# A decoder layer with 32 experts on one core: four late experts for three, earlier loads for the last norms, and 8 KB buffers

## The chip, the cores and the metric

The kernel runs on one core of a Trainium2 chip. The metric is the device time of one execution in microseconds. Three executions of the kernel before took 1423.0, 1424.0 and 1429.07 us; the median is 1424.0 us. TensorE is called PE, VectorE DVE, ScalarE ACT, GpSimd POOL and SyncE SP. SP issues the plain loads and stores; POOL issues the indirect ones (gathers and scatters by row index).

## The reference

The layer works on 1024 tokens of width 1024 in float32. First come a gated linear recurrence and a sliding-window attention over projections of x, mixed and normalised; their result is x1. Then comes the part that the change touches, cut here to what matters:

```
x = layer_norm(ALPHA*x + merged @ w_out)                      # x1
# each token: the best of 4 groups, then the best 2 of its 8 experts
h = silu(xb @ w_gate[e]) * (xb @ w_up[e])                     # per expert, 512 wide
y[token] += (h @ w_down[e]) * weight
x = layer_norm(ALPHA*x + y)                                   # the output
```

A token is in two experts of one group, so the last experts of different groups (7, 15, 23, 31) share no token.

## The kernel before

**Order.** The stages are attention and projections, the linear recurrence, the mixing with the first norm and the router, and the experts. From the mixing on, the order on each engine is the order in which the program is written out (all_order); every engine works in order and waits where an operand or a buffer isn't ready.

**Experts.** Each expert has at most 128 tokens in its first pass. Its weights come in 12 pieces: four of gate, four of up (each 2 x 128 rows of 512) and four of down (128 rows of 1024). first_pieces lists them for all experts: gate and up of expert e+1 come ahead of down of expert e, 384 pieces in all; the numbers of experts below are places in ORDER, so 29, 30 and 31 are the three of LAST. moe (from line 1238) walks over the pieces: at step i it splits piece i+3 (halve), does what has been put down for step i, multiplies piece i and issues one more load (fetch). A split gives a high and a low part: ACT casts (line 97), DVE subtracts (line 98). A product of split parts is three passes of PE (lines 102 to 104); a product of unsplit ones is one float32 matmul, which the trace shows as two passes (line 1165). The pieces from gate of expert 31 on are unsplit (first_whole).

**Loads.** fetch issues pieces in their order on SP. 29 are issued ahead; each later one waits until the piece eight before it has landed (DEEP, after). Loads, splits and the tiles of the end use one set of 36 buffers of 4 KB per partition (q4).

**Results.** turn_x gathers and transposes an expert's tokens; turn_h transposes its silu product hh. result scales the two halves of down's product and adds them to zd in memory by an indirect scatter with addition (line 1068); zd begins as x1. PSUM has four banks for products (mm): two for gate and up, two for down.

**The end.** final is put down for the piece after down of expert 28 and three more: it loads the norm's gain and shift (line 908), then block i of zd (z, line 1287) at step first + i, once all scatters into zd have landed. Eight steps later it puts the norm of block i down, 1.75 steps apart: a sum on ACT (line 1296), a square on ACT (line 1320), then gain on DVE with a power on POOL (lines 678, 679, 1324) and shift on DVE (line 1327) in the next two steps, and the store of the block. For each expert in LAST, finish takes the rows of zd that rows gathered (zf), adds the expert's product to them (line 1340), norms them in the same way and writes them over the stored blocks by index, after all eight stores (line 1343).

Of the kernel before, what the change touches and what calls it, by code (L numbers as in the profile page):

```python
# [23 lines left out]
LAST = (15, 23, 31)  # L24
# [36 lines left out]
class Builder:  # L61
# [5 lines left out]

    S2 = {"ob", "as", "aph", "apl", "ach", "acl", "oT", "hq", "hk", "hl", "hv", "hg", "hkd", "hkT", "hqb", "hst", "hE", "hS", "hsq", "ho",
          "rxT", "rlT", "hh", "hth", "htl"}
    NQ = 36  # L70
    NX = 9
    NRAW = 29
    LA = 3

    def __init__(self, tc, aps):
        self.tc, self.nc, self.a = tc, tc.nc, aps

    def tile(self, shape, dt, tag, bufs, name=None):
        name = name or tag
        if tag in self.S2:  # L80
            tag, bufs = "s2", self.n2
        pool = self.base if tag in ("q4", "st2", "base") else self.sb
# [4 lines left out]
    def q4(self, shape, dt=F32, name="q4"):  # L87
        return self.tile(shape, dt, "q4", self.NQ, name)

# [6 lines left out]
    def split(self, hi, lo, src, eng=None):  # L96
        self.nc.scalar.copy(hi, src)  # L97
        (eng or self.nc.vector).tensor_sub(lo, src, hi.bitcast(F32))  # L98

# [61 lines left out]
    def load_x(self, half, j):  # L161
        raw = self.q4([128, 2, 512], name="xr")
        self.nc.sync.dma_start(raw, self.a["xt"][half, j])
        return raw

    def split_x(self, half, raws):

        self.xh.append([])
        self.xl.append([])
        for raw in raws:  # L170
            h, l = self.q4([128, 2, 512], F32R, "xh"), self.q4([128, 2, 512], F32R, "xl")
            self.split(h, l, raw)
            self.xh[half].append(h)
            self.xl[half].append(l)
            yield
# [8 lines left out]
    def wload_half(self, c0, q):  # L184
        raw = self.q4([128, 4, 256], name=f"wr{c0}")
        self.nc.sync.dma_start(raw, self.a["w_in"][c0 // 256, q])
        return raw
# [4 lines left out]
    def wsplit_half(self, raw):  # L192
        h = self.q4([128, 4, 256], F32R, "wh")
        l = self.q4([128, 4, 256], F32R, "wl")
        self.split(h, l, raw)
        return h, l
# [45 lines left out]
    def att_proj(self):  # L242
# [11 lines left out]
        self.aq = [self.q4([128, 4, 256], name=f"aq{i}") for i in range(4)]  # L254
# [32 lines left out]
        self.ak = self.q4([128, T], name="ak")  # L287
# [394 lines left out]
    def mixing_loads(self):  # L682

        nc = self.nc
        self.stages, self.late_stages = {}, {}
        self.wab, self.ot, self.gates = {}, {}, {}
        wv = [self.a[nm].rearrange("(k p) c -> p k c", p=128) for nm in ("w_a", "w_b")]

        def load_wab(jt, when):
            raw = self.q4([128, 2, 4, 128], name="wab")  # L690
            for i in range(2):
                nc.sync.dma_start(raw[:, i], wv[i][:, :, jt * 128:jt * 128 + 128])
            self.at(2 * when, lambda: self.halves(self.wab, jt, raw), True)

        def load_o(b, half, nm, j):
            raw = self.q4([128, 2, 512], name=f"o{nm}")
            d = self.obd if nm == "b" else self.oad
            nc.sync.dma_start(raw, d.rearrange("k p t -> p k t")[:, 2 * j:2 * j + 2, half * 512:half * 512 + 512])
# [15 lines left out]
    def halves(self, dst, key, raw, eng=None):  # L714
        h, l = self.q4(raw.shape, F32R, "h"), self.q4(raw.shape, F32R, "l")
        self.split(h, l, raw, eng)
        dst[key] = h, l
# [23 lines left out]
    def mixing(self):  # L741
# [27 lines left out]
        def load_wo(b, p):  # L769
            raw = self.q4([128, 2, 512], name="wo")  # L770
            c, kp = p // 4, p % 4
            nc.sync.dma_start(raw, wov[:, 2 * kp:2 * kp + 2, c * 512:c * 512 + 512])
            self.at(2 * b + 2, lambda: halves(wo, p, raw, nc.gpsimd))
# [5 lines left out]
        def branch(half, jt):  # L779
            pss = []  # L780
            h, l = wab.pop(jt)
            for b, nm in enumerate("ab"):
                ps = self.bank("mm")
                for k in range(4):
                    oh, ol = ot[nm, k // 2]
                    self.mm3(ps, h[:, b, k], l[:, b, k], oh[:, k % 2], ol[:, k % 2], k == 0, k == 3)
                pss.append(ps)
                if b == 0:
                    yield
            if jt % 2 == 0:  # L790
                mg[jt // 2] = self.q4([128, 2, 512], F32R, "mh"), self.q4([128, 2, 512], F32R, "ml")
# [71 lines left out]
        for b in range(24, 31):  # L863
            for _ in range(2 if b % 2 else 1):
                at(before, b, lambda b: self.fetch())
# [3 lines left out]
        while tick < 2 * len(main) or stages or self.late_stages:  # L869
# [19 lines left out]
            if tick >= 2 * len(main) - 1:  # L889
                for _ in range(4 if tick < 2 * len(main) + 1 else 2):  # L890
                    self.fetch(True)
# [179 lines left out]
    def first_pieces(self):  # L1071
# [14 lines left out]
        self.first_whole = self.pieces.index((NE - 1, "w_g", 0))  # L1086
        self.raws, self.fetched = {}, []

    def whole(self, e, m):

        return self.pieces.index((e, m, 0)) >= self.first_whole

    def fetch(self, first=False):

        n = len(self.fetched)
        if n >= len(self.pieces) or first and n >= self.NRAW:
            return
        e, m, k = self.pieces[n]
        x = ORDER[e]
        if m == "w_d":  # L1100
            r = self.q4([128, 1, D], name="er")
            ins = self.nc.sync.dma_start(r, self.a[m][x].rearrange("(k p) c -> p k c", p=128)[:, k:k + 1])
        else:
            r = self.q4([128, 2, 512], name="er")
            ins = self.nc.sync.dma_start(r, self.a[m][x, k])
        if n >= self.DEEP:
            self.after(ins, self.fetched[n - self.DEEP])
        self.fetched.append(ins)
        self.raws[n] = r

    DEEP = 8
# [109 lines left out]
    def halve(self, i):  # L1221
        if i >= len(self.pieces):
            return
        e, m, k = self.pieces[i]
        raw = self.raws.pop(i)
        if i >= self.first_whole:
            self.V["w", e, m, k] = raw, None
            return
        h = self.q4(raw.shape, F32R, name="eh")
        l = self.q4(raw.shape, F32R, name="el")  # L1230
        self.split(h, l, raw)
        self.V["w", e, m, k] = h, l
# [5 lines left out]
    def moe(self):  # L1238
# [18 lines left out]
        self.final(at[NE - len(LAST) - 1, "w_d", 3] + 3)  # L1257
        for i in range(n):
# [9 lines left out]
            self.fetch()  # L1268
# [6 lines left out]
    def final(self, first):  # L1275
# [9 lines left out]
        def load(i):  # L1285
            z = self.q4([128, D], name="z")
# [3 lines left out]
        def rows(e):  # L1290
            self.zf[e] = self.q4([128, D], name="zf")
# [11 lines left out]
        for i in range(8):  # L1303
            self.step(first + i, lambda i=i: load(i))
            self.step(first + 8 + 1.75 * i, lambda i=i: self.norm2(self.zs[i], sums(i), lambda: store(i)))
        for j in range(len(LAST)):
            self.step(first + 8 + j, lambda j=j: rows(NE - len(LAST) + j))
        self.stored = int(first + 8 + 1.75 * 7) + 4

    def norm2(self, z, s, then):  # L1310
# [8 lines left out]
        def square():  # L1319
            nc.scalar.activation(self.q4([128, D], name="w"), z, AF.Square, bias=m, accum_out=v)  # L1320
# [59 lines left out]
    def more(self, e):  # L1380
# [16 lines left out]
        for nm in ("w_g", "w_u"):  # L1397
            ps = self.bank("mm")
            for k in range(8):
                w = self.st2()  # L1400
                nc.sync.dma_start(w, self.a[nm][bass.ds(e, 1), k // 2].rearrange("o p i c -> (o p) i c")[:, k % 2])
# [11 lines left out]
        wv = self.a["w_d"][bass.ds(e, 1)].rearrange("o (k p) c -> p (o k) c", p=128)  # L1413
        for j in range(2):
            ps = self.bank("mm")
            for k in range(4):
                w = self.st2()
                nc.sync.dma_start(w, wv[:, k, j * 512:j * 512 + 512])
# [37 lines left out]
def gate_up(w):  # L1456

    return np.ascontiguousarray(w.reshape(NE, 4, 2, 128, 512).transpose(0, 1, 3, 2, 4))


def arrays(inputs):
# [15 lines left out]
        "w_g": gate_up(f["w_exp_gate"][0]),  # L1477
        "w_u": gate_up(f["w_exp_up"][0]),
        "w_d": f["w_exp_down"][0],
# [18 lines left out]
```

## Time and profile before

| | |
|---|---|
| median of three executions | 1424.0 us |
| the profiled execution | 1423.78 us |
| its span, first to last instruction | 1421.9 us |
| PE busy | 1359.1 us (96%) |
| DVE busy | 1058.2 us (74%) |
| ACT busy | 792.3 us (56%) |
| POOL busy | 239.6 us (17%) |
| moved by DMA | 327.68 MB, 230 GB/s over the span |
| loads of expert weights | 384 of 512 KB |

Busy shares are means over stages with different limits. In 40 slices of the span PE is at 9 tenths or more in nearly all; the last three slices read 8, 4 and 4. The DMA engines read 9 from slice 25 on, and 9, 7 and 2 in the last three. A matmul's end is modelled, so busy PE can hold short waits; the distance between the starts of neighbouring passes is the better measure.

### The profile page before, as it was taken

How to read it: one execution, taken by the hardware profiler on the slowest of the kernel's cores; microseconds unless marked ns; L12 is line 12 of the kernel's file. 1: busy time of each engine (PE TensorE's matmuls, PEld its weight loads, DVE VectorE, ACT ScalarE, POOL GpSimd, SP SyncE). 2: the span in 40 equal slices, each digit the busy share in tenths (PEclk: the TensorE clock that was granted, in tenths of full speed). 3: DMA queues.
4: the chain of work that ended last, by engine and by line, in shares of the span. 5: the costliest groups of instructions: out<-in, count | busy, mean ns of one | idle time of the engine just before them, and what ended most of it. 6: DMA issues, size and time to landing. Idle time of an engine off the chain costs nothing. (4 is left out here: it accounts for less than half of the span.)

```text
span 1421.9 us, 20450 instructions
## 1 busy us (share of the span) xinstructions
PE 1359.1 (96%) x7162; PEld 1128.3 (79%) x7162; DVE 1058.2 (74%) x1654; ACT 792.3 (56%) x1282; POOL 239.6 (17%) x160
## 2 busy tenths in 40 slices
PE   7999999999999999999998999999999999999844
PEld 5888899988888888788787888888888888888721
DVE  4268977876666764857747889999999999999635
ACT  4367555434444442412201778888888888888533
POOL 0001221210010000410001112222222222222123
PEclk9999999999999999999999999999999999999967
DMA  6124223253334323774557899999999999999972
GB/s 254 56 89 156 88 92 105 67 173 116 126 108 136 111 88 103 240 252 137 174 195 277 314 361 369 370 359 349 360 349 359 357 359 360 360 359 361 370 264 95
DMA packets 142554, 327.68 MB, mean 230 GB/s; under 512 B 18614, under 2 KB 59702, under 8 KB 142448
## 3 DMA queue, kind: packets, MB, share of 16 engines
q1 hardware_dynamic: 132800, 308.78, 60.4%
q0 software_dynamic: 9648, 17.57, 4.8%
q8 instruction: 57, 0.93, 0.3%
q14 instruction: 49, 0.40, 0.1%
HBM read 291.43 MB, written 52.43 MB: 242 GB/s over the span
## 5 line engine op out<-in xcount | busy, mean ns | idle before, releaser
L98 DVE TENSOR_TENSOR el<-er,eh 128x1024 fp32r<-128x1024 f32 x368 | 436.5, 1221 | 53.7 <-ACT eh L97 38.1
L97 ACT CAST eh<-er 128x1024 fp32r<-128x1024 f32 x368 | 368.9, 1053 | 100.6 <-PE mm L103 83.5
L102 PE MATMUL mm<-xh,wh 128*128 128x512 f32 x480 | 198.3, 413 | 8.3 <-ACT wh L97 7.3
L102 PE MATMUL mm<-eh,xh 128*128 128x512 f32 x496 | 196.4, 396 | 0.0
L103 PE MATMUL mm<-el,xh 128*128 128x512 f32 x496 | 196.2, 395 | 0.0
L104 PE MATMUL mm<-eh,xl 128*128 128x512 f32 x496 | 196.1, 395 | 0.0
L103 PE MATMUL mm<-xl,wh 128*128 128x512 f32 x480 | 188.4, 393 | 0.8 <-DVE xl L98 0.8
L104 PE MATMUL mm<-xh,wl 128*128 128x512 f32 x480 | 189.0, 394 | 0.0
L104 PEld LDWEIGHTS mm<-eh,xl 128*128 128x128 f32 x496 | 93.2, 188 | 22.6
L103 PEld LDWEIGHTS mm<-el,xh 128*128 128x128 f32 x496 | 93.2, 188 | 22.3
L102 PEld LDWEIGHTS mm<-eh,xh 128*128 128x128 f32 x496 | 93.2, 188 | 22.3
L102 PEld LDWEIGHTS mm<-xh,wh 128*128 128x128 f32 x480 | 91.1, 190 | 24.2 <-ACT wh L97 7.3
L104 PEld LDWEIGHTS mm<-xh,wl 128*128 128x128 f32 x480 | 90.6, 189 | 20.6 <-DVE wl L98 0.8
L1064 POOL DMA_INDIRECT xg<-x1d,gi x32 | 58.1, 1814 | 279.3 <-PE pb L1127 236.3
L103 PEld LDWEIGHTS mm<-xl,wh 128*128 128x128 f32 x480 | 91.1, 190 | 16.0 <-DVE xl L98 1.4
L102 PE MATMUL mm<-eh,hth 128*128 128x512 f32 x240 | 100.2, 418 | 0.0
L1068 POOL DMA_INDIRECT zd<-y,gi x29 | 69.9, 2411 | 156.5 <-ACT y L1218 156.5
L104 PE MATMUL mm<-eh,htl 128*128 128x512 f32 x240 | 94.8, 395 | 0.0
L103 PE MATMUL mm<-el,hth 128*128 128x512 f32 x240 | 94.8, 395 | 0.0
L102 PE MATMUL mm<-wh,xh 128*128 128x256 f32 x256 | 73.1, 285 | 0.0
L104 PE MATMUL mm<-wh,xl 128*128 128x256 f32 x256 | 72.4, 283 | 0.0
L103 PE MATMUL mm<-wl,xh 128*128 128x256 f32 x256 | 72.4, 283 | 0.0
(257 smaller groups left out, 2566.6 us busy)
## 6 DMA issues: line engine op xcount, KB each, us to landing
er<-w_g SPq DMA_DIRECT2D x128, 512.0 KB, 12.5
er<-w_u SPq DMA_DIRECT2D x128, 512.0 KB, 12.5
er<-w_d SPq DMA_DIRECT2D x128, 512.0 KB, 12.0
wr<-w_in SPq DMA_DIRECT2D x38, 512.0 KB, 4.4
gated<-st SPq DMA_DIRECT2D x32, 256.0 KB, 2.1
st<-gated SPq DMA_DIRECT2D x32, 256.0 KB, 2.7
xr<-xt SPq DMA_DIRECT2D x8, 512.0 KB, 7.6
wab<-w_a SPq DMA_DIRECT2D x16, 256.0 KB, 3.7
```

The source lines that it names most:

```text
L97: self.nc.scalar.copy(hi, src)
L98: (eng or self.nc.vector).tensor_sub(lo, src, hi.bitcast(F32))
L102: mm(out, lh, rh, start=start, stop=False)
L103: mm(out, lh, rl, start=False, stop=False)
L104: mm(out, ll, rh, start=False, stop=stop)
L1064: self.nc.gpsimd.indirect_dma_start(to, None, rows, bass.IndirectOffsetOnAxis(ap=self.column(self.gi, e), axis=0), bounds_check=T - 1, oob ...
L1068: self.nc.gpsimd.indirect_dma_start(self.zd, bass.IndirectOffsetOnAxis(ap=idx, axis=0), y, None, bounds_check=T - 1, oob_is_err=False, com ...
```

## The change

- LAST holds 7, 15, 23, 31, so four experts (places 28 to 31) are finished by norm and indirect write, and 28 scatter into zd.
- Buffers are 18 of 8 KB (q8) for 36 of 4 KB. A 4 KB tile with a pair key shares a buffer with the next of the same key; a split's high and low part share one; before, each had its own.
- Expert weights lie in memory in blocks of 1 MB, 8 KB per partition, and a load brings two pieces. 14 loads are issued ahead for 29 of half the size; a load waits for the fourth before it in place of the eighth.
- Unsplit are gate, up and down of expert 31 and gate and up of 30; down of 30 is split.
- final starts after down of expert 27, at that piece. Blocks of zd are loaded from first + 6, that is among the last four weight loads, rows are gathered from first + 6, norms start at first + 14 and stand 3 steps apart. The sums' and squares' outputs that nobody reads go to x4 tiles.
- Six loads of 1 MB are issued late in the mixing, where ten of 512 KB were.

The core of the diff:

```
-LAST = (15, 23, 31)
+LAST = (7, 15, 23, 31)
-    NQ = 36
+    NQ = 18
-    NRAW = 29
+    NRAW = 14
+    def q4(self, shape, pair, dt=F32):
+        if pair in self.pairs:
+            t = self.pairs.pop(pair)[:, 1024:2048]
+        else:
+            t = self.pairs[pair] = self.q8([128, 2048], dt, str(pair[0]))
+            t = t[:, 0:1024]
+        return self.shaped(t, shape)
+    def halved(self, src, eng=None):
+        hi, lo = self.parts(src.shape)
+        self.split(hi, lo, src, eng)
+        return hi, lo
+    def parts(self, shape):
+        t = self.q8([128, 2048], F32R, "hl")
+        return self.shaped(t[:, 0:1024], shape), self.shaped(t[:, 1024:2048], shape)
...
-        return self.pieces.index((e, m, 0)) >= self.first_whole
+        return e == NE - 1 or e == NE - 2 and m != "w_d"
...
-        if n >= len(self.pieces) or first and n >= self.NRAW:
+        if 2 * n >= len(self.pieces) or first and n >= self.NRAW:
...
+        e, m, k = self.pieces[2 * n]
+        r = self.q8([128, 2, D] if m == "w_d" else [128, 4, 512], name="er")
+        ins = self.nc.sync.dma_start(r, self.a[m][ORDER[e], k // 2])
...
-    DEEP = 8
+    DEEP = 4
...
-        self.final(at[NE - len(LAST) - 1, "w_d", 3] + 3)
+        self.final(at[NE - len(LAST) - 1, "w_d", 3])
...
-            self.fetch()
+            if i % 2:
+                self.fetch()
...
-            nc.scalar.activation(self.q4([128, D], name="w"), self.zs[i], AF.Copy, accum_out=s)
+            nc.scalar.activation(self.x4(name="w"), self.zs[i], AF.Copy, accum_out=s)
...
-            self.step(first + i, lambda i=i: load(i))
-            self.step(first + 8 + 1.75 * i, lambda i=i: self.norm2(self.zs[i], sums(i), lambda: store(i)))
+            self.step(first + 6 + i, lambda i=i: load(i))
+            self.step(first + 14 + 3 * i, lambda i=i: self.norm2(self.zs[i], sums(i), lambda: store(i)))
...
-            self.step(first + 8 + j, lambda j=j: rows(NE - len(LAST) + j))
-        self.stored = int(first + 8 + 1.75 * 7) + 4
+            self.step(first + 6 + j, lambda j=j: rows(NE - len(LAST) + j))
+        self.stored = first + 14 + 3 * 7 + 3
...
+def blocks(w):
+    n = 2048 // w.shape[2]
+    return np.ascontiguousarray(w.reshape(NE, 2, n, 128, w.shape[2]).transpose(0, 1, 3, 2, 4))
```

## Rows read from the trace of the kernel before

**Rows 1.** Busy time by stretches of the span; the first line names the columns.
```profile
core 0: us, PE busy (x) PEld busy (x) DVE busy (x) ACT busy (x) POOL busy (x), PEclk, DMA share, GB/s
800.00:905.00 105.00, 105.00 (x486) 85.47 (x485) 94.84 (x92) 85.35 (x104) 20.04 (x10) 1.00 1.00 364
905.00:1346.00 441.00, 441.00 (x2052) 359.43 (x2051) 394.99 (x386) 355.94 (x433) 104.80 (x49) 1.00 0.99 359
1346.00:1369.70 23.70, 0.57 (x4) 0.14 (x2) 0.15 (x1) 2.92 (x6) 0.00 (x0) 0.61 0.99 378
1369.70:1375.00 5.30, 5.30 (x7) 2.21 (x8) 3.33 (x6) 4.23 (x8) 3.31 (x2) 0.50 0.17 70
...
1406.00:1421.90 15.90, 0.03 (x1) 0.00 (x0) 5.47 (x9) 1.24 (x2) 4.30 (x5) 0.60 0.13 48
```

**Rows 2.** Timeline of POOL, 1305 to 1345: start, duration, line, operation [idle before].
```profile
1312.88 2.47 POOL L1068 DMA_INDIRECT zd<-y,gi  x1 [5.00 <-ACT y L1218]
1330.87 1.57 POOL L1068 DMA_INDIRECT zd<-y,gi  x1 [15.52 <-ACT y L1218]
```

**Rows 3.** Timeline of SP's queue: issues of weight loads and of z.
```profile
905.12 5.41 SPq L1105 DMA_DIRECT2D er<-w_g  x4
...
1327.88 4.81 SPq L1105 DMA_DIRECT2D er<-w_g  x4
...
1341.13 11.78 SPq L1102 DMA_DIRECT2D er<-w_d  x8
...
1356.34 9.19 SPq L1287 DMA_DIRECT2D z<-zd  x8
```

**Rows 4.** Timeline of ACT, 1338 to 1372.
```profile
1339.88 1.05 ACT L97 CAST eh<-er 128x1024 fp32r<-128x1024 f32 x1 [1.94 <-DMA er<-w_d]
1366.50 1.06 ACT L1296 ACTIVATE w<-z 128x1024 f32<-128x1024 f32 x1 [25.57 <-DMA z<-zd]
...
1369.08 1.05 ACT L1136 COPY xh<-pb 128x512 f32<-128x512 f32 x2
```

**Rows 5.** Timeline of PE, 1324 to 1329 and from 1365 on.
```profile
1328.29 0.40 PE L102 MATMUL mm<-eh,xh 128*128 128x512 f32 x1
1328.99 0.40 PE L102 MATMUL mm<-eh,xh 128*128 128x512 f32 x1
...
1369.69 6.75 PE L1165 MATMUL mm<-er,xh 128*128 128x512 f32 x9 [23.13 <-ACT xh L1136]
...
1386.15 5.31 PE L1165 MATMUL mm<-er,hth 128*128 128x512 f32 x12
1395.10 0.80 PE L1149 MATMUL pb<-const,hh 128*128 128x128 f32 x4 [3.64 <-DVE fv L678]
```

**Rows 6.** Groups by line: whole span, then 1340 to 1422; busy us, mean ns, idle before.
```profile
L98 DVE TENSOR_TENSOR el<-er,eh 128x1024 fp32r<-128x1024 f32 x368 | 436.5, 1221 | 53.7 <-ACT eh L97 38.1
...
L679 POOL TENSOR_TENSOR fv<-fv,mhalf 128x1 f32<-128x1 f32 x11 | 14.5, 1322 | 41.7 <-DVE fv L678 41.6
L1327 DVE SCALAR_TENSOR_TENSOR z<-z,fv,ln_b 128x1024 f32<-128x1024 f32 x8 | 10.3, 1284 | 2.9 <-POOL fv L679 2.9
...
L1320 ACT ACTIVATE w<-z,fm 128x1024 f32<-128x1024 f32 x8 | 9.2, 1149 | 7.6 <-DVE fm L1317 5.3 <-issue 2.3
L1296 ACT ACTIVATE w<-z 128x1024 f32<-128x1024 f32 x8 | 8.4, 1048 | 25.6 <-DMA z<-zd 25.6
```

**Rows 7.** DMA queues, 800 to 1337: packets, MB, share of 16 engines' time.
```profile
q1 hardware_dynamic: 48712, 177.37, 87.7%
```

**Rows 8.** DMA queues, 8 to 12 us; the packets under 512 B carry no data.
```profile
DMA packets 466, 1.69 MB, mean 422 GB/s; under 512 B 54, under 2 KB 54, under 8 KB 466
q1 hardware_dynamic: 466, 1.69, 103.1%
```

**Rows 9.** DMA queues, 98 to 100 us.
```profile
DMA packets 288, 0.52 MB, mean 262 GB/s; under 512 B 32, under 2 KB 32, under 8 KB 288
q1 hardware_dynamic: 288, 0.52, 70.4%
```

More of the change, by code (lines that the diff above doesn't have):

```diff
@@ L76, in __init__ @@
         self.tc, self.nc, self.a = tc, tc.nc, aps
+        self.pairs = {}
     def tile(self, shape, dt, tag, bufs, name=None):
@@ L81, in tile @@
             tag, bufs = "s2", self.n2
-        pool = self.base if tag in ("q4", "st2", "base") else self.sb
+        pool = self.base if tag in ("q8", "st2", "base") else self.sb
         if tag == "base":
@@ L85, in tile, with q8, shaped @@
         return pool.tile(list(shape), dt, name=name, tag=tag, bufs=bufs)
-    def q4(self, shape, dt=F32, name="q4"):
-        return self.tile(shape, dt, "q4", self.NQ, name)
+    def q8(self, shape, dt=F32, name="q8"):
+        return self.tile(shape, dt, "q8", self.NQ, name)
+    def q4(self, shape, pair, dt=F32):
[5 more added lines that the diff above has]
+        return self.shaped(t, shape)
+    @staticmethod
+    def shaped(t, shape):
+        if len(shape) == 2:
+            return t
+        names = "abc"[:len(shape) - 1]
+        return t.rearrange("p (%s) -> p %s" % (" ".join(names), " ".join(names)), **{n: k for n, k in zip(names, shape[1:])})
     def st2(self, shape=(128, 512)):
@@ L161, in load_x @@
     def load_x(self, half, j):
-        raw = self.q4([128, 2, 512], name="xr")
+        raw = self.q4([128, 2, 512], ("xr", half, j // 2))
         self.nc.sync.dma_start(raw, self.a["xt"][half, j])
@@ L170, in split_x @@
         for raw in raws:
-            h, l = self.q4([128, 2, 512], F32R, "xh"), self.q4([128, 2, 512], F32R, "xl")
-            self.split(h, l, raw)
+            h, l = self.halved(raw)
             self.xh[half].append(h)
@@ L184, in wload_half @@
     def wload_half(self, c0, q):
-        raw = self.q4([128, 4, 256], name=f"wr{c0}")
+        raw = self.q4([128, 4, 256], ("wr", c0))
         self.nc.sync.dma_start(raw, self.a["w_in"][c0 // 256, q])
@@ L192, in wsplit_half @@
     def wsplit_half(self, raw):
[L193 to L196, printed above, removed]
+        return self.halved(raw)
     def proj_T(self, w, ct, half):
@@ L253, in att_proj @@
         raw3 = self.wload(2560)
-        self.aq = [self.q4([128, 4, 256], name=f"aq{i}") for i in range(4)]
+        self.aq = [self.q4([128, 4, 256], ("aq", i // 2)) for i in range(4)]
         def keep(ps, ch, ct, half):
@@ L286, in att_proj @@
         w = self.wsplit(raw3)
-        self.ak = self.q4([128, T], name="ak")
+        self.ak = self.q4([128, T], ("ak",))
         self.av = self.tile([128, 8, 2, 2, 64], F32R, "av", 1)
@@ L689, in load_wab @@
         def load_wab(jt, when):
-            raw = self.q4([128, 2, 4, 128], name="wab")
+            raw = self.q4([128, 2, 4, 128], ("wab", jt // 2))
             for i in range(2):
-                nc.sync.dma_start(raw[:, i], wv[i][:, :, jt * 128:jt * 128 + 128])
+                self.nc.sync.dma_start(raw[:, i], wv[i][:, :, jt * 128:jt * 128 + 128])
             self.at(2 * when, lambda: self.halves(self.wab, jt, raw), True)
         def load_o(b, half, nm, j):
-            raw = self.q4([128, 2, 512], name=f"o{nm}")
+            raw = self.q4([128, 2, 512], ("o", nm))
             d = self.obd if nm == "b" else self.oad
-            nc.sync.dma_start(raw, d.rearrange("k p t -> p k t")[:, 2 * j:2 * j + 2, half * 512:half * 512 + 512])
+            self.nc.sync.dma_start(raw, d.rearrange("k p t -> p k t")[:, 2 * j:2 * j + 2, half * 512:half * 512 + 512])
             self.at(2 * b + 2, lambda: self.halves(self.ot, (nm, j), raw))
@@ L714, in halves @@
     def halves(self, dst, key, raw, eng=None):
-        h, l = self.q4(raw.shape, F32R, "h"), self.q4(raw.shape, F32R, "l")
-        self.split(h, l, raw, eng)
-        dst[key] = h, l
+        dst[key] = self.halved(raw, eng)
     def mixing_start(self):
@@ L769, in load_wo @@
         def load_wo(b, p):
-            raw = self.q4([128, 2, 512], name="wo")
+            raw = self.q4([128, 2, 512], ("wo", p // 2))
             c, kp = p // 4, p % 4
-            nc.sync.dma_start(raw, wov[:, 2 * kp:2 * kp + 2, c * 512:c * 512 + 512])
+            self.nc.sync.dma_start(raw, wov[:, 2 * kp:2 * kp + 2, c * 512:c * 512 + 512])
             self.at(2 * b + 2, lambda: halves(wo, p, raw, nc.gpsimd))
@@ L790, in branch @@
             if jt % 2 == 0:
-                mg[jt // 2] = self.q4([128, 2, 512], F32R, "mh"), self.q4([128, 2, 512], F32R, "ml")
+                mg[jt // 2] = self.parts([128, 2, 512])
             def post():
@@ L863, in mixing @@
         for b in range(24, 31):
-            for _ in range(2 if b % 2 else 1):
+            if b != 27:
                 at(before, b, lambda b: self.fetch())
@@ L889, in mixing @@
             if tick >= 2 * len(main) - 1:
-                for _ in range(4 if tick < 2 * len(main) + 1 else 2):
+                for _ in range(2 if tick < 2 * len(main) + 1 else 1):
                     self.fetch(True)
@@ L1085, in first_pieces @@
         d(NE - 1)
-        self.first_whole = self.pieces.index((NE - 1, "w_g", 0))
         self.raws, self.fetched = {}, []
     def whole(self, e, m):
-        return self.pieces.index((e, m, 0)) >= self.first_whole
+        return e == NE - 1 or e == NE - 2 and m != "w_d"
     def fetch(self, first=False):
         n = len(self.fetched)
-        if n >= len(self.pieces) or first and n >= self.NRAW:
+        if 2 * n >= len(self.pieces) or first and n >= self.NRAW:
             return
[L1098 to L1105, printed above, removed]
+        e, m, k = self.pieces[2 * n]
+        r = self.q8([128, 2, D] if m == "w_d" else [128, 4, 512], name="er")
+        ins = self.nc.sync.dma_start(r, self.a[m][ORDER[e], k // 2])
         if n >= self.DEEP:
@@ L1223, in halve @@
             return
[L1224 to L1232, printed above, removed]
+        raw = self.raws[i // 2]
+        n = raw.shape[1] // 2
+        raw = raw[:, n * (i % 2):n * (i % 2) + n]
+        self.V[("w",) + self.pieces[i]] = (raw, None) if self.whole(*self.pieces[i][:2]) else self.halved(raw)
     def step(self, at, fn):
@@ L1285, in load @@
         def load(i):
-            z = self.q4([128, D], name="z")
+            z = self.q4([128, D], ("z", i // 2))
             nc.sync.dma_start(z, self.zd[i * 128:i * 128 + 128, :])
@@ L1290, in rows @@
         def rows(e):
-            self.zf[e] = self.q4([128, D], name="zf")
+            self.zf[e] = self.q4([128, D], ("zf", e // 2))
             self.gather_rows(self.zf[e], self.zd, e)
@@ L1319, in square @@
         def square():
-            nc.scalar.activation(self.q4([128, D], name="w"), z, AF.Square, bias=m, accum_out=v)
+            nc.scalar.activation(self.x4(name="w"), z, AF.Square, bias=m, accum_out=v)
         def gain():
@@ L1400, in more @@
                 w = self.st2()
-                nc.sync.dma_start(w, self.a[nm][bass.ds(e, 1), k // 2].rearrange("o p i c -> (o p) i c")[:, k % 2])
+                nc.sync.dma_start(w, self.a[nm][bass.ds(e, 1), k // 4].rearrange("o p i c -> (o p) i c")[:, k % 4])
                 nc.tensor.matmul(ps, xT[:, k], w, start=k == 0, stop=k == 7)
@@ L1412, in more @@
         y = self.x4()
-        wv = self.a["w_d"][bass.ds(e, 1)].rearrange("o (k p) c -> p (o k) c", p=128)
         for j in range(2):
@@ L1417, in more @@
                 w = self.st2()
-                nc.sync.dma_start(w, wv[:, k, j * 512:j * 512 + 512])
+                wv = self.a["w_d"][bass.ds(e, 1), k // 2].rearrange("o p i c -> (o p) i c")
+                nc.sync.dma_start(w, wv[:, k % 2, j * 512:j * 512 + 512])
                 nc.tensor.matmul(ps, hT[:, k], w, start=k == 0, stop=k == 3)
@@ L1453, in build @@
                     self.moe()
-def gate_up(w):
-    return np.ascontiguousarray(w.reshape(NE, 4, 2, 128, 512).transpose(0, 1, 3, 2, 4))
+def blocks(w):
+    n = 2048 // w.shape[2]
+    return np.ascontiguousarray(w.reshape(NE, 2, n, 128, w.shape[2]).transpose(0, 1, 3, 2, 4))
 def arrays(inputs):
@@ L1476, in arrays @@
         "b_r": np.concatenate([f["router_group_b"][0], f["router_expert_b"][0]]),
-        "w_g": gate_up(f["w_exp_gate"][0]),
-        "w_u": gate_up(f["w_exp_up"][0]),
-        "w_d": f["w_exp_down"][0],
+        "w_g": blocks(f["w_exp_gate"][0]),
+        "w_u": blocks(f["w_exp_up"][0]),
+        "w_d": blocks(f["w_exp_down"][0]),
         "ln2_g": f["ln2_g"][0],
```

## The prediction

> **What bounds the kernel now.** I read the busy times by stretch first, then the DMA queue's own timeline, then the tail of the timeline engine by engine. The reader is to see in them two stages with different limits.
>
> From 800 us to 1346 us TensorE (PE) is busy without a gap, and the DMA engines are too (share 0.99 to 1.00) [rows 1]. An expert takes PE 18.0 us (the step between two scatters, 1312.88 to 1330.87) [rows 2], but its weights take longer to arrive: from the loads of w_g at 905.12 to those at 1327.88 lie 22 experts, so 19.2 us each [rows 3]. The 29 pieces loaded ahead hide this 1.2 us per expert until they are used up: at 1339.88 ScalarE (ACT) waits 1.94 us for a w_d piece [rows 4]. So the weight stream and PE reach the end of the stage together, and the stream sets what comes then.
>
> After 1346 PE is hardly busy for 23.7 us [rows 1]. ACT works in order, and the first sum of final (line 1296) stands on it ahead of the copies of xh for the last expert (line 1136). The sum waits 25.57 us for z of block 0 [rows 4]; z was issued at 1356.34, behind all weights on SyncE (SP) [rows 3]; PE waits 23.13 us for xh [rows 5]. From z0's landing (1366.4, just ahead of the sum's start) to the end of the span (1421.9) it is 55.5 us. The execution took 1423.78 us, 1.9 us more than its span and 0.2 under the median of 1424.0; I add 1.9 to every end of span below.
>
> **The change part by part.** With LAST of four, final begins at piece 343, not 358. Loads of z stand at steps 349 to 356, norms at 357 to 378. Pieces 356 to 363 are gate and up of expert 30, 364 to 367 down of 29, 368 to 375 gate and up of 31, 376 to 379 down of 30, 380 to 383 down of 31.
>
> *1. Where z0 lands, at today's rate.* z0 no longer waits for the down weights of 30 and 31: eight pieces of 0.52 MB, at the 360 GB/s of this stage 1.45 us each, 11.6 us [rows 1]. The loads of ln2_g and ln2_b stay ahead of it. So z0 lands at 1366.4 - 11.6, about 1355. Its wait for the scatter of expert 27 (issued 1312.88 [rows 2]) costs nothing. Three z loads and one weight load alternate behind it; the last down weights then land some 22 us after z0, before PE needs them.
>
> *2. From z0 to the end.* It is no longer the last expert that stands behind the first sum, but two. At step 357 ACT sits in sum 0; silu of 30 and the splits of down 29 (steps 361 to 364) are behind it, and on VectorE (DVE) the finish of 28, which holds two of the four PSUM banks. PE can still do gate and up of 30 (unsplit now, so ACT owes it nothing): 8 pieces of two products, each product two passes of 0.43 (twelve take 5.31, the last one's overlapping end included), 1.72 us a piece [rows 5], 13.8 us from 1328.3 to about 1342. Then it waits. After z0:
> - before the first split, ACT has two sums (1.05 us) and the squares of 0, 28 and 1 (1.15), some 6.5 us with their read-outs; the square of 1 waits for DVE, where the finish of 28 and two pairs of 1.28 us steps, for 0 and 28, stand ahead: 12 us in all [rows 6];
> - down of 29: PE alone 5.6 us (two products of 0.70 a piece [rows 5]), but paced by DVE, which has four splits of 1.22 and two norms of 2.9 (two 1.28 steps and small ones) between, then the product hh that PE's next transposes wait for: 14 us [rows 6];
> - gate and up of 31, unsplit: 13.8 us;
> - down of 30, which is split after the change: paced like 29's, 14 us;
> - down of 31, eight products of 0.86: 6.9 us;
> - from PE's end to the end of the span, as now: 15.9 us [rows 1].
> Sum 76.6 us. At today's rate the end is thus 1355 + 76.6 = 1431.6, 10 us later than now: z0 comes 11 us earlier, and 21 us more stand behind it. The two 14s are bounded by 5.6 below (PE alone) and by 17 above (a third norm of 2.9 falls between the splits); so the sum lies between 60 and 83. After a wait the granted clock stands at 0.50, the lower level, for 5.3 us now [rows 1]; after the change this falls on down of 29, where DVE sets the pace, so I add nothing for it.
>
> *3. The floor.* If z0 lands by about 1330, its 12 us lie beside gate and up of 30, and PE sets the end: 1328.3 + 13.8 + 14 + 13.8 + 14 + 6.9 + 15.9 = 1406.7. PE also pays for unsplit against split products, 16 x (0.86 - 0.70) less 8 of the same, 1.3 us, contained in these terms.
>
> *4. The rate of the weight stream* decides between the two. Pieces become 1 MB with 8 KB per partition in place of 4 KB; bytes in flight stay 4 MB (four for eight). In the stage the hardware queue fills 87.7% of 537 us for 177.37 MB, 174 ns per 4 KB on one of 16 engines [rows 7]. No row shows an 8 KB packet of this queue, so I take it from two sizes on full engines. At 8 to 12 us, 412 packets of 4 KB took 1.031 of 64 engine-us: 160 ns each [rows 8]. At 98 to 100 us, 256 of 2 KB took 0.704 of 32: 88 ns [rows 9]; those are stores, so the pair is only near. Twice 88 less 160 is 16 ns that belong to a packet and not to its bytes. One packet fewer per 8 KB saves 8 ns per 4 KB, 4.6% of 174. The bounds are 0 (the stage is held by something that sees bytes alone) and 8%, the way from 174 to the 160 of the quiet stretch; below 0 is possible too (a coarser piece lands later), 1%. I take 4%. One per cent of the queue's 471 us is 4.7 us of lead at the end, so 4% lets z0 land 19 us earlier, at 1336: 1336 + 76.6 = 1412.6, and 1.9 makes 1414.5.
>
> The Trainium skill speaks against that gain: DMA: Bandwidth & Descriptors (Bandwidth, on where 436 GB/s comes from) says that loads from HBM are bound by the HBM side at about 358 GB/s per core. By that rule the sum is today's rate, 1433.5. The stage's 360 GB/s agrees with it [rows 1], the 422 GB/s at 8 to 12 us does not [rows 8].
>
> *5. Edits that cost nothing, or little.* One scatter of y less and one gather of zf more: both on GpSimd (POOL), off the path, some 1 us of DMA either way. One norm more (expert 28's): in term 2. 192 loads for 384: SP has slack, it waits for landings. Sums' scratch in x4 tiles: short-lived, nine buffers. Pairs in 8 KB buffers before the experts: a buffer is held until both halves are done, and ak wastes half of one; by my count of live buffers the attention, scan and mixing stages reach 17 or 18 of 18 where they had up to 36 of 36. PE is bound there by its own products; if the cover is gone, a load waits for a split, 0 to 4 us in all. I take 0. Weights ahead of the first expert: 28 pieces for 29, 1.4 us of lead, inside the uncertainty of 4.
>
> **The rivals.** *A: the stream is not quicker (slower).* One mechanism: ACT in order behind sum 0. If 8 KB rows bring under 1%, z0 lands at 1350 to 1355, and with 76.6 and 1.9 the time is 1429 to 1434; I price it at 1433. It decides from where z0 lands after 1352. For it: the stage's rate sits at 356 to 364 GB/s whatever runs beside it [rows 1]. Against it: the same 4 KB packets went at 422 [rows 8].
>
> *B: no change.* Half of the gain, 2.1%: z0 at 1345, the end 1345 + 76.6 = 1421.6, 1423.5. For it: stores of 2 KB may carry a dearer overhead than loads do. Against it: nothing in the rows, it lies between the ends.
>
> *C: PE to the floor.* Gain above 5%, or norms that cost DVE less than 14 us beside a split: 1406.7 + 1.9, 1408.6, down to 1402 if one wait for hh goes too. For it: today's wait of PE before the transposes of hh is 3.64 us, no more [rows 5]. Against it: each norm goes from ACT to DVE, back to ACT, to POOL (1.32 us) and to DVE again, all in order [rows 6].
>
> **How the numbers follow.** The forecast, 2.5% to 5% quicker loads, ends between 1410 and 1421, at 1414.5: 0.38. Rival C 0.10, B 0.27, A 0.25. What a measurement of this kernel tells from no change is about 0.5%, 7 us: faster ends under 1417, slower above 1431. Of the forecast's 0.38 some 0.36 lies under 1417; with C's 0.10 that is 0.46 faster; A 0.25 slower; the rest, 0.29, within. The range goes from C's 1404 to 1437, A with 4 us for the tighter buffers; the likeliest case alone has 1409 to 1421.
>
> **What would show it.** Right: w_g loads of neighbouring experts under 18.7 us apart late in the stage, the queue under 168 ns per 4 KB, z0 landing between 1330 and 1342, ACT's longest wait for z0 about 6 us where it was 25.57, PE idle before down of 29 for some 6 us and not before gate and up of 31. Wrong: loads still 19.2 us apart and z0 at 1355, with PE waiting over 20 us for a split of down 29 (A); from z0's landing to the end far from 77 us, which would break term 2; or experts that begin some microseconds later than now, which would put a cost on the tighter buffers.

## The result and the profile after

The kernel after takes 1435.2 us (median of 6 runs, 1432.5 to 1437.1) where the kernel before takes 1423.9: a ratio of 1.0072, interval 1.0054 to 1.009. The change makes it slower by 0.7%; the forecast was 1414.5, and the time is inside the range, 2 us over rival A's price of 1433. The profiled execution took 1435.7, its span is 1433.7.

The busy times by stretch, as in [rows 1]:

```profile
core 0: us, PE busy (x) PEld busy (x) DVE busy (x) ACT busy (x) POOL busy (x), PEclk, DMA share, GB/s
800.00:905.00 105.00, 105.00 (x488) 85.46 (x487) 95.08 (x93) 85.70 (x103) 18.73 (x10) 1.00 0.99 364
905.00:1343.80 438.80, 435.71 (x1993) 349.45 (x1991) 380.26 (x371) 343.49 (x417) 97.01 (x50) 1.00 0.98 361
1343.80:1363.90 20.10, 0.04 (x1) 0.04 (x1) 6.84 (x14) 6.95 (x12) 2.92 (x2) 0.58 1.02 416
1363.90:1415.30 51.40, 40.64 (x112) 24.13 (x112) 36.37 (x53) 25.72 (x41) 13.29 (x9) 0.83 0.25 99
1415.30:1433.70 18.40, 0.00 (x0) 0.00 (x0) 5.47 (x9) 1.24 (x2) 5.09 (x5) 0.59 0.13 48
```

The stage of the experts moves 361 to 364 GB/s, where before it moved 359 to 364. PE's empty stretch is still there, 20 us long in place of 23.7, but it now lies ahead of down of 29, with 51 us of PE's work behind it, 41 of them busy.

The DMA queues from 800 to 1337 us (packets, MB, share of 16 engines), beside [rows 7]:

```profile
q1 hardware_dynamic: 24498, 177.70, 86.2%
q0 software_dynamic: 8601, 15.80, 11.8%
```

Half the packets, and hardly less time: 170.7 ns per 4 KB (86.2% of 16 engines for 537 us, over 177.70 MB) in place of 174, 1.9%. SP's queue shows that the loads came no faster for it (issue, duration):

```profile
904.93 0.33 SPq L1121 DMA_DIRECT2D er<-w_g  x1
...
1326.91 0.33 SPq L1121 DMA_DIRECT2D er<-w_g  x1
...
1337.97 0.37 SPq L1300 DMA_DIRECT2D z<-zd  x1
```

The w_g loads of 22 experts lie 422.0 us apart, 19.2 each, as in [rows 3]; z is issued 18 us earlier than before. ACT's timeline (idle time before, and what ended it, in brackets), beside [rows 4]:

```profile
1353.54 1.06 ACT L1309 ACTIVATE w<-z 128x1024 f32<-128x1024 f32 x1 [24.25 <-DMA z<-zd]
...
1362.78 1.03 ACT L115 CAST hl<-er 128x1024 fp32r<-128x1024 f32 x1
1363.71 0.59 ACT L1217 ACTIVATE hh<-mm 128x512 f32<-128x512 f32 x1
```

z0 is there at 1353.5, but ACT reached the sum earlier too, so it waits nearly as long as before (24.25 us for 25.57); and behind the sum now stand the first split of down of 29 (1362.78) and silu of expert 30 (1363.71). PE, beside [rows 5]:

```profile
1329.90 13.89 PE L1181 MATMUL mm<-er,xh 128*128 128x512 f32 x32
1363.86 0.80 PE L130 MATMUL mm<-hl,hth 128*128 128x512 f32 x1 [20.06 <-ACT hl L115]
...
1377.29 0.86 PE L1165 MATMUL pb<-const,hh 128*128 128x128 f32 x4 [4.47 <-DVE fm L1330]
...
1380.50 14.13 PE L1181 MATMUL mm<-er,xh 128*128 128x512 f32 x32
...
1404.63 1.11 PE L1165 MATMUL pb<-const,hh 128*128 128x128 f32 x4 [5.74 <-DVE fm L1330]
...
1408.11 7.12 PE L1181 MATMUL mm<-er,hth 128*128 128x512 f32 x16
```

It has done gate and up of 30 at 1343.8, waits 20.06 us, and then twice more for hh behind norms on DVE. At the end POOL has writes between its powers (L1356 is the indirect write, L703 the power):

```profile
1412.83 1.58 POOL L1356 DMA_INDIRECT out<-zf,gi  x1 [5.05 <-issue]
1416.90 0.99 POOL L1356 DMA_INDIRECT out<-zf,gi  x1 [2.49 <-DMA out<-zf,gi]
1417.89 0.60 POOL L703 TENSOR_TENSOR fv<-fv,mhalf 128x1 f32<-128x1 f32 x1
1420.82 1.03 POOL L1356 DMA_INDIRECT out<-zf,gi  x1 [2.33 <-DVE zf L1353]
1423.15 1.47 POOL L703 TENSOR_TENSOR fv<-fv,mhalf 128x1 f32<-128x1 f32 x1 [1.30 <-DVE fv L702]
1426.23 1.01 POOL L1356 DMA_INDIRECT out<-zf,gi  x1 [1.61 <-DVE zf L1340]
```

The power for expert 30 (1417.89) stands behind two writes, the second of which waits for the first one's landing; DVE waits 5.04 us for it. In the kernel before one write stood there, and DVE waited 1.56 us:

```profile
1406.86 1.28 DVE L1327 SCALAR_TENSOR_TENSOR zf<-zf,fv,ln_b 128x1024 f32<-128x1024 f32 x1 [1.56 <-POOL fv L679]
```

### The profile page after: what moved, and what is told of

The parts are those of the page before. It is cut to its first block, busy times and chain, and to the rows that moved or that the text cites. A ratio compares the mean times of both kernels' runs of the same rounds, so it can differ in the third digit from the quotient of the medians.

```text
span 1433.7 us, 19671 instructions
## 1 busy us (share of the span) xinstructions
PE 1362.7 (95%) x7154; PEld 1129.7 (79%) x7154; DVE 1058.9 (74%) x1657; ACT 790.8 (55%) x1278; POOL 231.5 (16%) x162
## 5 line engine op out<-in xcount | busy, mean ns | idle before, releaser
L116 DVE TENSOR_TENSOR hl<-er,hl 128x1024 fp32r<-128x1024 f32 x364 | 431.5, 1220 | 64.4 <-ACT hl L115 62.0
L115 ACT CAST hl<-er 128x1024 fp32r<-128x1024 f32 x364 | 368.4, 1054 | 102.0 <-PE mm L132 99.8
L130 PE MATMUL mm<-hl 128*128 128x512 f32 (+1 forms) x992 | 373.6, 377 | 9.2 <-ACT hl L115 8.5
L132 PE MATMUL mm<-hl 128*128 128x512 f32 (+1 forms) x992 | 362.2, 365 | 2.6 <-DVE hl L116 2.6
L131 PE MATMUL mm<-hl 128*128 128x512 f32 (+1 forms) x992 | 360.9, 364 | 0.8 <-DVE hl L116 0.8
L130 PEld LDWEIGHTS mm<-hl 128*128 128x128 f32 x992 | 188.0, 189 | 37.4 <-ACT hl L115 10.1
L132 PEld LDWEIGHTS mm<-hl 128*128 128x128 f32 x992 | 187.5, 189 | 36.5 <-DVE hl L116 6.6
L131 PEld LDWEIGHTS mm<-hl 128*128 128x128 f32 x992 | 188.1, 190 | 25.4 <-DVE hl L116 1.3
L130 PE MATMUL mm<-hl,xh 128*128 128x512 f32 x480 | 190.1, 396 | 0.0
L131 PE MATMUL mm<-hl,xh 128*128 128x512 f32 x480 | 189.8, 395 | 0.0
L132 PE MATMUL mm<-hl,xl 128*128 128x512 f32 x480 | 189.7, 395 | 0.0
L130 PE MATMUL mm<-hl,hth 128*128 128x512 f32 x248 | 106.0, 427 | 20.1 <-ACT hl L115 20.1
L132 PEld LDWEIGHTS mm<-hl,xl 128*128 128x128 f32 x480 | 90.2, 188 | 21.8
L130 PEld LDWEIGHTS mm<-hl,xh 128*128 128x128 f32 x480 | 90.2, 188 | 21.6
L131 PEld LDWEIGHTS mm<-hl,xh 128*128 128x128 f32 x480 | 90.2, 188 | 21.6
L131 PE MATMUL mm<-hl,hth 128*128 128x512 f32 x248 | 99.8, 402 | 0.5 <-DVE fv L702 0.5
L132 PE MATMUL mm<-hl,htl 128*128 128x512 f32 x248 | 99.6, 401 | 0.0
```

The source lines that it names most:

```text
L130: mm(out, lh, rh, start=start, stop=False)
L131: mm(out, lh, rl, start=False, stop=False)
L132: mm(out, ll, rh, start=False, stop=stop)
```

## Experiments

Two questions: what each half of the change costs, and what sets the end once z is there. Ratios are against the kernel before. Code cuts show the lines that matter; `...` stands for what is left out.

**1. The rows by themselves.** Only loads, in pieces of three shapes with 4.2 MB in flight, executed once:

```
for nm, shape, depth in (("w_g", [128,2,512], 8), ("w_u", [128,4,512], 4), ("w_d", [128,512], 16)):
    ... nc.sync.dma_start(r, w[e, k])   # each waits for the one `depth` before it
```

> Only loads, nothing else of the computation: 67 MB in rows of 4 KB per partition (pieces of 0.52 MB, eight in flight), then 67 MB in rows of 8 KB (1.05 MB, four in flight), then 67 MB in rows of 2 KB (0.26 MB, sixteen in flight). Theory T, a DMA engine's time goes by bytes: the 4 KB and the 8 KB stretch run at the same rate within 1%, at the 405 to 420 GB/s of the quiet stretches of the trace after, 160 to 166 us each, and one engine takes 160 ns for 4 KB and 320 for 8. Rival R, packets have a fixed part of 16 ns (my term 4) which the stage then lost elsewhere: 8 KB rows are 5% quicker than 4 KB (304 ns), 2 KB rows 10% slower (88 ns).

Windows inside the three stretches, 4 KB, 8 KB and 2 KB per partition:

```profile
core 0: us, DVE busy (x) POOL busy (x), PEclk, DMA share, GB/s
20.00:150.00 130.00, 0.00 (x0) 0.00 (x0) 1.00 1.03 410
200.00:310.00 110.00, 0.00 (x0) 0.00 (x0) 1.00 1.01 422
380.00:490.00 110.00, 0.00 (x0) 0.00 (x0) 1.00 1.05 387
```

Between both theories. By these rates 16 engines need 159.8, 155.3 and 169.3 ns per 4 KB, so a packet has a fixed part of 9 ns (9.5 from 2 to 4 KB, 9.0 from 4 to 8): an 8 KB row saves 2.9%, where nothing else uses the engines. My 16 was worked out from the share of the engines' time that the packets take, not from a rate. By that measure (102.7, 101.3 and 105.3% in the queue view) the three take 164, 157 and 179 ns, a fixed part of 14 and a saving of 4.3%. But a share over 100% means that recorded times of packets overlap, so they add up to more than the packets cost.

The Trainium skill (DMA: Bandwidth & Descriptors, Bandwidth) names about 10.5 ns per packet, in a note on its smallest transfer. There it is the whole time shared out among 64 packets, so it is not this fixed part, and no run here tests it.

**2 and 3. Each half alone.** First the kernel after with the schedule of before (the steps of the gathers and writes go back with it):

```
-LAST = (7, 15, 23, 31)                 +LAST = (15, 23, 31)
-self.final(at[...])                    +self.final(at[...] + 3)
-first + 6 + i / first + 14 + 3 * i     +first + i / first + 8 + 1.75 * i
-return e == NE - 1 or e == NE - 2 and m != "w_d"
+return e == NE - 1 or e == NE - 2 and m == "w_d"
```

> The kernel after with the buffers of 8 KB and the 1 MB loads kept, and the schedule of before: three last experts, final at piece 358, z, norms and unsplit pieces where they were. Theory T (8 KB rows bring nothing, the whole loss is the schedule with ACT in order behind sum 0): as before within 0.2%, 1421 to 1425 us, z0's sum starts at 1364 to 1367. Rival R (the quicker loads are there but a coarser piece and tighter buffers give them back): off 1424 by 3 us or more, with experts that begin later or a w_g spacing off 19.2 us.

1419.8 us, 0.9967 (0.9951 to 0.9983): faster by 4.5 us; z0's sum starts at 1362.70, 3.8 us earlier than in [rows 4]. Then the same edits the other way round, on the kernel before with its 4 KB buffers:

> The kernel before on its 4 KB buffers and 0.5 MB loads, with the schedule alone: four last experts, final at piece 343, z from step 349, norms from 357 every 3 steps, down of 30 split, sums' scratch in x4. Theory T: 1433 to 1438 us, as the kernel after; z0's sum starts at 1353 to 1356 and PE waits about 20 us before down of 29. Rival R: under 1430, since part of the loss then belongs to the 8 KB pieces.

1441.3 us, 1.0123 (1.0102 to 1.0145): slower by 17 us; the sum starts at 1355.68 and PE waits 24.02 us before down of 29:

```profile
1365.99 0.79 PE L102 MATMUL mm<-eh,hth 128*128 128x512 f32 x1 [24.02 <-ACT eh L97]
```

So the schedule costs 17, and the 8 KB rows give back 4.5 (on the old schedule) to 6 (on the new, 1441.3 to 1435.2). Neither theory had that: the 8 KB rows do help, by far less than they save alone. They come with 1 MB pieces and paired buffers here; no run parts the three.

**4. The norms later, alone.**

```
-self.step(first + 14 + 3 * i, ...norm2...)
+self.step(first + 27 + 1.75 * i, ...norm2...)
-self.stored = first + 14 + 3 * 7 + 3
+self.stored = first + 27 + 12 + 3
```

> The kernel after with the eight norms 13 steps later and closer (step 370 + 1.75 i in place of 357 + 3 i); loads of z, gathers and everything else stay. Theory T (ACT's first sum stands ahead of the splits of down 29): the splits no longer wait for z0, PE goes from gate and up of 30 at 1344 through down of 29 at once, gate and up of 31 end at about 1364, PE ends near 1380 and the kernel at 1400 to 1410 us. Rival D (DVE has 8 x 2.9 us of norms and 4 x 4.6 of finishes, and POOL a power in each: the chain of twelve norms sets the end wherever it stands): 1425 to 1435 us, the time that PE gains turns up as a longer tail.

1422.8 us, 0.9992 (0.9975 to 1.0008): 12.5 us less than after, and 13 to 23 more than theory T asked for. PE of this run:

```profile
1328.68 13.89 PE L1181 MATMUL mm<-er,xh 128*128 128x512 f32 x32
1342.01 0.80 PE L130 MATMUL mm<-hl,hth 128*128 128x512 f32 x1
1345.38 0.72 PE L131 MATMUL mm<-hl,hth 128*128 128x512 f32 x1 [2.58 <-DVE hl L116]
...
1380.88 1.11 PE L1165 MATMUL pb<-const,hh 128*128 128x128 f32 x4 [5.74 <-DVE hh L1221]
...
1387.29 10.10 PE L1181 MATMUL mm<-er,hth 128*128 128x512 f32 x16 [2.73 <-ACT hth L1170]
```

The 20 us wait is gone, so it came from the place of the norms, with the first sum ahead on ACT. But the norms now stand beside down of 30 and delay hh of 31, and on POOL the last power (ready when DVE ends line 702 at 1401.7) starts at 1410.67:

```profile
1402.23 1.57 POOL L1356 DMA_INDIRECT out<-zf,gi  x1 [5.06 <-issue]
1406.28 0.99 POOL L1356 DMA_INDIRECT out<-zf,gi  x1 [2.48 <-DMA out<-zf,gi]
1409.69 0.96 POOL L1356 DMA_INDIRECT out<-zf,gi  x1 [2.43 <-DMA out<-zf,gi]
1410.67 0.59 POOL L703 TENSOR_TENSOR fv<-fv,mhalf 128x1 f32<-128x1 f32 x1
```

Rival D's 1425 to 1435 is missed as well, but half of it came true: once the first wait was gone, a second limit left a gain of 12.5 us and no more.

**5. Six pieces in flight.**

```
-DEEP = 4
+DEEP = 6
```

> The kernel after with six 1 MB pieces in flight where it has four. In the stage of the experts the hardware queue of after fills 86.0% and the software queue 11.9%, 98.2% together, where before had 99.3%. Theory G (part of the 2.9% that an 8 KB row saves by itself is lost in gaps, since four pieces of 1 MB drain unevenly): the sum of the shares goes back over 99%, the rate from 360 to 363 or more, z0's sum starts 3 to 5 us earlier than 1353.5, and the kernel takes 1430 to 1433 us. Rival (the rest is taken by the scatters' own traffic, the gaps are none of the depth): rate 360, z0 at 1353 to 1354, 1434 to 1437 us.

366 GB/s from 905 to 1300 us where after has 360, so four pieces in flight hold the rate back; the engines are filled to 98.7%, not 99, so how much of that is gaps stays open. But z0 comes no earlier (1353.94): z is issued at 1332.61 and stands behind six pieces, so that 21.3 us pass to its sum, where after has 15.6 (from 1337.97 to 1353.54). In this execution, the slowest of its four, the first gather of the experts also stands 4.2 us later than in after (785.84 for 781.67), so its trace doesn't price the depth. 1433.3 us, 1.006 (1.0044 to 1.0077), not to be told from after.

**6. Without the scatters.**

```
-self.accumulate(self.column(self.gi, e), y)
+if e in (0, NE - len(LAST) - 1):
+    self.accumulate(self.column(self.gi, e), y)
```

> The kernel after without the scatters of y, but for experts 0 and 27 of the order: the sums over experts are left out, all else stays. Theory Q (the software queue's 11.9% is what keeps the loads from the 422 GB/s that 8 KB rows reach alone): the software queue falls to 5% or less, the loads go up to 385 GB/s or more, w_g loads are 18.1 us apart (PE's own pace), z0's sum starts at 1340 or earlier. Rival (the stage is held at 360 GB/s whoever moves the bytes): the rate stays at 360, spacing at 18.4 to 19, z0 at 1345 to 1350.

The queues from 905 to 1300 us, in after and then without the scatters:

```profile
q1 hardware_dynamic: 17881, 130.20, 86.0%
q0 software_dynamic: 6229, 11.54, 11.9%
```

```profile
q1 hardware_dynamic: 18889, 137.56, 92.6%
q0 software_dynamic: 3168, 5.91, 4.1%
```

The queue of the weights moves 5.7% more. w_g loads are 18.1 us apart (904.75 to 1303.10, 22 experts), PE's own pace, so the rate of both queues stays at 364 GB/s and my 385 was wrong. But no load waits for another to land any more; from 905 to 1300 us SP waits for PE alone (us in total, times, longest), where in after it waits 327 us for earlier loads to land:

```profile
SPq L1121 <- PE mm L132: 340.1, 131, 3.3
```

The shares still add up to 97%, so a full share does not by itself show that the engines are the limit. The sum of z0 starts at 1329.08, PE does not stop before down of 29, and the kernel takes 1412.3 us (one run) on the schedule of after. Theory Q holds but for its 385: scatters keep the loads from PE's pace. They take 7.8% of the engines for 5.63 MB, 359 ns per 4 KB.

**7 and 8. Two other places for the norms.** On the 8 KB buffers with the schedule of before, the norms stand behind the copies that PE needs:

```
-first + 8 + 1.75 * i
+first + 11 + 1.75 * i
```

The step of the writes moves by three as well.

> The 8 KB buffers with the schedule of before, three last experts, and one edit: the eight norms 3 steps later (369 + 1.75 i in place of 366 + 1.75 i), so that the copies of xh and hth for the last experts stand ahead of the first sum on ACT. Theory T (the cost is PE's work queued behind a sum that waits): z0 lands at 1362 as it did, but gate and up of 31 and down of 30 run beside that wait; PE ends near 1375 to 1385 and the kernel at 1403 to 1412 us. Rival D (from z0 the twelve or eleven norms on DVE, then three writes in series, set the end): DVE has 8 x 2.9 and 3 x 4.6 us, 37 us from 1363 at best, so the end at 1363 + 37 + 16 = 1416, no more than 4 us under the 1419.8 of the 8 KB buffers alone.

1420.2 us, 0.9969 (0.9958 to 0.9979), the same as without this edit. Gate and up of 31 begin at 1345.85, where experiment 2 has 1365.83; then PE waits 7.94 and 11.87 us, and the last power starts at 1409.59 behind two writes. Then the kernel after with z loaded early:

```
-first + 6 + i        +first + (3, 3, 4, 4, 6, 6, 8, 8)[i]
-first + 14 + 3 * i   +first + (19, 21, 24, 25, 27, 28, 30, 32)[i]
-if i % 2:
+for _ in range(0 if i in (345, 347, 349, 351) else 2 if i in (353, 355, 357, 359) else i % 2):
     self.fetch()
-first + 6 + j         +first + (6, 6, 8, 8)[j]
-self.stored = first + 14 + 3 * 7 + 3
+self.stored = first + 40
```

> The kernel after with z loaded ahead of four late weight pieces (steps 346 to 351; the weights follow two at a time from 353), gathers of zf at 349 and 351, and each norm at a step where ACT and DVE owe PE little: 362, 364, 367, 368, 370, 371, 373, 375; writes from 383. Theory T with D: z0 lands near 1340, before ACT wants it, so nothing stands behind a wait; norms fill the stretches of unsplit gate and up; the last z is stored by about 1385, PE ends at 1380 to 1390, the kernel at 1398 to 1410 us. Rival: the weights that were moved behind 4 MB of z now come late (gate and up of 31 wait), or the norms' chain is as long as ever: 1415 to 1425 us.

1422.5 us, 0.9991 (0.998 to 1.0002). z0 is there at 1346.2, not 1340; PE waits 4.69, 4.22 and 4.53 us for DVE, and the last power starts at 1409.62. Three arrangements that start the norms at 1346, 1357 and 1366 all end at 1420 to 1423. That is what rival D expects: the chain of work on DVE and POOL behind z sets the end. Experiments 9 to 12 test it.

**9. What holds PE.** After, with the downs of 29 and 30 as whole products:

```
-return e == NE - 1 or e == NE - 2 and m != "w_d"
+return e >= NE - 2 or e == NE - 3 and m == "w_d"
```

> The kernel after with the downs of experts 29 and 30 done as whole products (as gate, up and down of 31 are), so that ACT and DVE owe PE no split after step 355; norms, loads and all else as in after. It asks what of ACT's queue behind sum 0 holds PE. Theory T1 (the splits of down 29): PE goes on through down of 29 at 1344 without waiting for z0, and the kernel takes 1410 to 1420 us. Theory T2 (silu of 30 and the finish of 28, which free the PSUM banks that down of 29 needs, stand behind sum 0 just as well): PE still waits some 11 to 14 us, to 1355 to 1358, and only the pacing by splits goes (2 x 7 us of PE's waits beside DVE): 1422 to 1430 us.

```profile
1353.09 3.39 PE L1181 MATMUL mm<-er,hth 128*128 128x512 f32 x4 [10.35 <-ACT w L1309]
```

PE still waits for z0's sum (1350.97), with no split left that it could need: theory T2, though the PSUM bank as the reason is read from the program and was not tried alone. 1421.4 us, 0.9989 (0.9976 to 1.0002), just under T2's range: 13.8 us less than after, of which z0's earlier landing is 2.6. I put the rest down to the splits that DVE and ACT no longer do, which this run doesn't show apart.

**10 to 12. Taking work from DVE, and changing POOL's order.** The edit of experiment 9 and that of experiment 8 together, with ln_g and ln_b loaded three steps earlier and the norms at first + (21, 23, 25, 26, 28, 29, 31, 32):

> z loaded early as in the run before of that name, with the downs of 29 and 30 as whole products, ln_g and ln_b loaded three steps earlier (339), and norms at steps 364, 366, 368, 369, 371, 372, 374, 375. Theory D (since z0 is there in time, the chain of DVE work sets the end: twelve norms, 8 x 2.9 and 4 x 4.6 us, beside it eight splits of 1.2; then writes in series): DVE has 11 us less to do and the finish of 28 no longer waits for ln_g, so the last z is stored by 1385, PE ends near 1385, the kernel at 1400 to 1410 us. Rival E (the four writes, 3.5 us each after the last store of z, with the last power behind them on POOL, set the end by themselves): 1416 to 1422 us, the last power again at about 1410.

1410.2 us, 0.9903 (0.9882 to 0.9923): at the upper end of theory D's range. The last z is stored from 1378.8; PE's one long wait is 8.73 us before hh of 31. Then the edit of experiment 9 with the norms of experiment 4:

> The kernel after with the norms later (370 + 1.75 i) and the downs of 29 and 30 as whole products; z is loaded where after loads it. Theory D: the chain of norms begins at z0's landing, 1350 to 1354 as before, and loses the splits beside it, 5 to 6 us after z0: 1413 to 1418 us in place of 1422.75. Rival E: no change, 1420 to 1424 us.

1414.9 us, 0.9936 (0.9915 to 0.9958), as D said; 7.9 us less than experiment 4, from the splits alone. In experiment 10 the last power still stood behind writes:

```profile
1386.01 1.45 POOL L703 TENSOR_TENSOR fv<-fv,mhalf 128x1 f32<-128x1 f32 x1 [8.54 <-DVE fv L702]
1387.65 2.06 POOL L1356 DMA_INDIRECT out<-zf,gi  x1 [0.19 <-issue]
1392.20 0.99 POOL L1356 DMA_INDIRECT out<-zf,gi  x1 [2.49 <-DMA out<-zf,gi]
1396.11 0.97 POOL L1356 DMA_INDIRECT out<-zf,gi  x1 [2.92 <-issue]
1397.09 0.59 POOL L703 TENSOR_TENSOR fv<-fv,mhalf 128x1 f32<-128x1 f32 x1
```

Hence the last edit, on top of experiment 10:

```
-self.stored = first + 40
+self.stored = first + 36
```

> The early z with whole downs, and one edit: the writes of experts 28 and 29 stand on POOL ahead of the power of expert 30 (step 379 in place of 383). In the run before they stood between the powers of 30 and 31: the power of 31 was ready at 1392.7 and began at 1397.1 behind three writes in series. Theory W (the serial writes on POOL are part of the path): the two writes go into POOL's idle stretch from 1378 on, as soon as the last z is stored (about 1382), the power of 30 begins up to 2 us later, that of 31 some 3 us earlier, and the kernel takes 1405 to 1408 us in place of 1410.2. Rival F (the writes wait for the store of the last z, which lands too late, and now hold the power of 30 as well): 1410 to 1413 us.

```profile
1381.59 1.05 POOL L1356 DMA_INDIRECT out<-zf,gi  x1 [5.05 <-issue]
1385.12 0.99 POOL L1356 DMA_INDIRECT out<-zf,gi  x1 [2.48 <-DMA out<-zf,gi]
1386.11 1.19 POOL L703 TENSOR_TENSOR fv<-fv,mhalf 128x1 f32<-128x1 f32 x1
1389.04 1.03 POOL L1356 DMA_INDIRECT out<-zf,gi  x1 [1.74 <-DVE zf L1340]
1392.88 1.47 POOL L703 TENSOR_TENSOR fv<-fv,mhalf 128x1 f32<-128x1 f32 x1 [2.81 <-DVE fv L702]
```

1406.5 us, 0.9886 (0.9858 to 0.9915), in theory W's range. The last power starts 4.2 us earlier and stands behind no write, the time falls by 3.7. The intervals of the two runs overlap, and z0 came 0.9 us earlier, which the edit doesn't touch, so it is the trace that speaks for W, and the size of the gain stays rough. This version beats both kernels, the one before by 1.1%.

## Why the prediction was wrong

*The step that failed is 4*, the 4% by which the weight stream was to be quicker; 0.3% came of it (129.83 to 130.20 MB on the queue of the weights, from 905 to 1300 us). The w_g spacing stayed at 19.2 us. z0's sum started at 1353.5 where I had 1336, which is 17.5 of the 20.7 us that I missed by.

The gain was lost in three places. I had priced a packet by its own recorded time, 16 ns, from a pair of which one half were stores; loads alone show 14 by that measure, and 9 by the rate, so 2.9% (experiment 1). In the stage the queue's own time per byte fell by 1.9%. And most of that did not become rate: the software queue took 0.5 points more (11.4% to 11.9%), and the engines were filled to 98.2% where it had been 99.3%. Experiments 5 and 6 show that the depth of four pieces and the scatters held the rate. The 4.7 us per per cent, on the other hand, hold roughly: experiment 2 moved 0.9% more weights in that stretch and gained 3.8 us at z0.

*Step 1 was right*: 1355 at today's rate, 1353.5 measured.

*Step 2 was right within 4 us*: 80.2 from z0 to the end of the span where I had 76.6. By terms, predicted and measured: to the first split 12 and 9.3; down of 29 with hh 14 and 17.7, over its upper bound of 17; gate and up 13.8 and 13.6; down of 30 14 and 14.0; down of 31 6.9 and 7.1; tail 15.9 and 18.5. The tail missed 2.6: with four experts POOL has one more write ahead of the power of expert 30, and DVE waits 5.04 us there for 1.56. On 4 KB buffers (experiment 3) the same way took 82.0 us (1355.68 to 1437.7).

*Step 3* came near where z was there in time: without the scatters z0's sum started at 1329 and the time was 1412.3 (one execution), beside 1408.6 for rival C. A z0 as early as the forecast wanted thus gives about its time, but the missing scatters brought z0 that early, not the rows. Where z0 came at 1346 (experiment 8), the time was 1422.5.

*Step 5 was right*: the first gather of the experts stands at 781.67 us where it was 783.51, so the tighter buffers cost nothing that shows.

*Rival A was what happened*, by its mechanism and near its price: 1433 against 1435.2. The price is partly luck: it describes the schedule without any gain from the rows, and that schedule alone took 1441.3 (experiment 3), 8 us more; the 8 KB rows then took 6 off. Its reading of the row that mattered (the rate stays at 356 to 364 whatever runs beside it) was evidence I gave 0.25. The rule of the Trainium skill (DMA: Bandwidth & Descriptors, where 436 GB/s comes from) gave 1433.5 and was right on the time, but not on the reason: loads from HBM alone ran at 422 GB/s on this core (experiment 1), and without the scatters the loads kept up with PE. So 360 was what remained beside another queue with four pieces in flight, and not a limit of HBM.

## What to carry to other kernels

Price a change of packet size by the rate that it gives, not by the packets' recorded times, which overlap. Then ask what the busy stage leaves of that gain: who else uses the engines, and how many pieces are in flight. Before an operation that waits for a transfer is moved earlier in an engine's order, list what stands behind it there. When the first wait is removed, look for the next chain at once: here three placements ended at 1420 to 1423 us, until work was taken from DVE and the writes were moved out of the way of the last powers on POOL.

## What the hardware showed unexpectedly

By the recorded times of packets, an indirect write that adds cost the engines 359 ns per 4 KB (experiment 6), more than twice the 171 ns of a load in the stage of the kernel after. The gathers that stay in experiment 6 took 180 (4.1% for 5.91 MB). Two indirect writes to the same tensor that stand next to each other on POOL start 3.4 to 4.6 us apart (1406.28 and 1409.69 in experiment 4, 1387.65 and 1392.20 in experiment 10), since in this program the second waits for the first to land, and what stands behind them on POOL waits as well.
